# Norm sums by column in a kernel's closing stages, and products of half the tokens ahead of the other half's statistics

## The chip, the cores and the metric

The kernel runs on one core of one Trainium2 chip. The metric is the time of one execution on the device in microseconds (us), less being better. Its engines are TensorE (PE, with its weight loads as PEld), VectorE (DVE), ScalarE (ACT), GpSimd (POOL) and SyncE (SP); each works through its own queue of instructions in order, and semaphores tie the queues together.

## The reference: what is computed

Two layers over 256 latent tokens `x_l` and 256 context tokens `x_c`, 1024 wide, in float32. Each layer normalises, mixes tokens by four branches, adds, normalises again, and runs a feed-forward network with a short convolution over the tokens:

```python
def rmsnorm(x, g):
    xf = x.astype(jnp.float32)
    y = xf * lax.rsqrt(jnp.mean(xf * xf, axis=-1, keepdims=True) + NORM_EPS)
    return (y * g.astype(jnp.float32)).astype(x.dtype)

def modulate(h, shift, scale):
    return h * (1.0 + scale) + shift

def conv_ffn(h, p):
    u = dwconv(h @ p['w_up'], p['ffn_conv_w'], p['ffn_conv_b'], (FFN_CONV - 1) // 2)
    g, v = jnp.split(u, 2, axis=-1)
    return (jax.nn.silu(g) * v) @ p['w_down']

def layer(x_l, x_c, c, c_ctx, p, cos, sin, lambda_init, with_ctx_out):
    mod_l = (jax.nn.silu(c) @ p['w_ada'] + p['b_ada'])[:, None, :]
...
    h_l = modulate(rmsnorm(x_l, p['norm1_g']), sh1_l, sc1_l)
    h_c = modulate(rmsnorm(x_c, p['norm1_g']), sh1_c, sc1_c)
    y_l, y_c = token_mixer(h_l, h_c, p, cos, sin, lambda_init, with_ctx_out)
    x_l = x_l + g1_l * y_l
    x_l = x_l + g2_l * conv_ffn(modulate(rmsnorm(x_l, p['norm2_g']), sh2_l, sc2_l), p)
    if not with_ctx_out:
        return x_l, None
...
```

In the second layer the context tokens end after the mixer's keys and values; its last stages work on the latent tokens alone. The result is `x_l`.

## The kernel before

**Layout.** The tokens stand as columns: `x` is `xm` [128, 8, 512], eight blocks ("columns" below, k or j) of 128 of the 1024 features by 512 tokens; tokens 0 to 255 are the latent ones (`v` = 0), 256 to 511 the context ones (`v` = 1).

**Products.** Each factor is split into a high and a low part (`Mat`, `split`, L253): ScalarE or VectorE makes the high part (a cast, L256), VectorE or GpSimd subtracts it to get the low part (L251). A product is three TensorE matmuls (`mm3`, L267 to L269: low x high, high x low, high x high). The text ahead counts such matmuls, each 128x256 or 128x512, when it says "products". `fm` (L525) runs k over the eight columns for one tile of 128 outputs; with `halves` it does the context tokens first, then the latent ones. Results lie in PSUM in four buffers `big` and four `small`.

**Weights** are loaded by SyncE's queue (`wcols`, `wraw`) into two buffers, and split into four buffers `whl`. `turn[1]` says whose turn it is for the low part: GpSimd every `turn[1]`th time, VectorE else; `NEVER` keeps it on VectorE.

**A norm.** `norm_stats` (L497) squares each column on ScalarE (L503, L506) and adds the squares up on VectorE (L507). `rstd` (L477) sums over the partitions by two small matmuls with ones (L484), scales on VectorE (L487), takes the power -1/2 on GpSimd (L489), and spreads the result over the partitions by two matmuls (L493). `norm` (L511) then makes `h` column by column: times the broadcast (L517, VectorE), scale and shift (L519 ScalarE for odd columns, L521 VectorE for even ones), and the split into `hh` (ScalarE, L256) and `hl` (L251, VectorE for every fourth column, GpSimd else). The temporary `fo` has three buffers. The scale and shift come from `norm_coeffs` (L455).

**Closing stages.** `closing` (L1107) makes the last product of a mixer ("out") or of a feed-forward network ("down3") for four columns at a time, context tokens first, and adds it to `x` (L1119). A norm of `x` follows at three places, called A, B and C from here on: A, the end of layer 0's mixer into `norm2` and the products `up0` and `up1`; B, the end of layer 0's feed-forward network into `norm1` of layer 1 and the products `rgx0` and `rgx1` (`rg_in`, L989); C, the end of layer 1's mixer (latent tokens alone) into `norm2` and `up0`.

**Filler.** While layer 0's feed-forward network runs, a `Filler` (L411) makes layer 1's modulation: 48 blocks of weights `wa` are loaded by ScalarE's queue into two buffers, multiplied by the conditioning row `crow` and summed, for the latent vector on VectorE (L435), for the context one on GpSimd (L431) and ScalarE (L432). `crow` itself is made by `cond` (L291 to L303). The filler is handed out in shares between the feed-forward tiles.

**What sets the order.** The Python code emits the instructions; a planner then places them in each engine's queue by simulated time, within the dependences. `tc.high_priority()` puts what is emitted inside it ahead of what is ready at the same time; `tc.issue_after(i)` keeps what is inside from being placed before instruction `i`. `after[l, j0]` (L1120) holds the last residual update of a half of a closing stage for that use.

Of the kernel before, what the change touches and what calls it, by code (L numbers as in the profile page):

```python
# [14 lines left out]
OP = mybir.AluOpType  # L15
# [192 lines left out]
def _build(ctx, nc, tc, I, out, dbg):  # L208
# [56 lines left out]
    def mm3(ps, a, b, start, stop):  # L265

        PE.matmul(ps, a.l, b.h, start=start, stop=False)  # L267
        PE.matmul(ps, a.h, b.l, start=False, stop=False)  # L268
        PE.matmul(ps, a.h, b.h, start=False, stop=stop)  # L269
# [241 lines left out]
    def norm(x, rs, a, sh):  # L511
        h = Mat(*(hp.tile([128, KT, T], F32R, name=f"h{i}") for i in "hl"))
        for v, r in rs.items():
            ts = slice(v * 256, v * 256 + 256)
            for k in range(KT):
                t = tt("fo", 256)
                V.tensor_tensor(t, x[:, k, ts], r, op=OP.mult)  # L517
                if k % 2:
                    S.activation(t, t, AF.Identity, scale=a[:, k, v:v + 1], bias=sh[:, k, v:v + 1])  # L519
                else:  # L520
                    V.tensor_scalar(t, t, a[:, k, v:v + 1], sh[:, k, v:v + 1], op0=OP.mult, op1=OP.add)  # L521
                split(h[:, k, ts], t, V if k % 4 == 3 else G)
        return h

    def fm(ps, w, h, n, start=True, stop=True, halves=False):  # L525

        if halves and n > 256:
            for v in reversed(range(n // 256)):
                ts = slice(v * 256, v * 256 + 256)
                fm(ps[:, ts], w, h[:, :, ts], 256)  # L530
            return
        kn = w.h.shape[1]
        for k in range(kn):
            mm3(ps, w[:, k], h[:, k, :n], start and k == 0, stop and k == kn - 1)
# [20 lines left out]
    class Mixer:  # L555
# [433 lines left out]
        def rg_in(self, i, tag, bufs):  # L989

            l, p, h = self.l, self.p, self.h
            w = wcols(l, f"rgx{i}")
            xr = self.long([128, 2, T], tag, bufs)
            bws = []
            for c in range(2):
                cp = 2 * i + c
                ps = big()
                fm(ps, w[c], h, T, halves=True)
# [108 lines left out]
    def closing(l, name, acts, x, g, n, fill=None):  # L1107

        kn = len(acts)
        for j0 in range(0, 8, 4):  # L1110
# [12 lines left out]

    def ffn(l, p, x, h, n, last, fp, fill=None):
        def up(f0, f1):
            acts = []
            for i in range(f0, f1):
                turn[1] = NEVER if i < 2 else 2
                w = wcols(l, f"up{i}")
                o = []  # L1130
                for s in range(2):
                    ps = big(n)
                    fm(ps, w[s], h, n, halves=i < 2)
# [13 lines left out]
        def down(g, acts, fin):  # L1147
            f0, f1 = FGROUPS[g]
            if g == len(FGROUPS) - 1 and not fin:
                closing(l, f"down{g}_", acts, x, g2, n)  # L1150
                return
# [26 lines left out]
        down(len(FGROUPS) - 1, prev, last)  # L1178
# [54 lines left out]
    for l in range(DEPTH):  # L1233
        full = l < DEPTH - 1
        if l:
            p = load_params(l)
            with tc.high_priority():
                r = norm_stats(x, T)
        with tc.issue_after(after[0, 4]) if l else nullcontext():
            a1, sh1 = norm_coeffs(p, mods[l], 0, "norm1", 1, 2)  # L1240
        h = norm(x, r, a1, sh1)
# [8 lines left out]
        rin = [mx.rg_in(0, "bcm", 1), mx.rg_in(1, "xs", 2)]  # L1250
# [64 lines left out]
        closing(l, "out", ms, x, g1, n, fill and (lambda: fill.share(0.5)))  # L1315
# [6 lines left out]
        with tc.high_priority():  # L1322
            h = norm(x, norm_stats(x, n), a2, sh2)
# [5 lines left out]
        ffn(l, p, x, h, n, not full, fp, fill)  # L1329
# [17 lines left out]
```

## Time and profile before

| | |
|---|---|
| time, median of 3 runs (lowest to highest) | 1796.97 us (1796.64 to 1797.96) |
| the profiled execution | 1793.63 us, its span 1791.8 us |
| TensorE busy | 1695.5 us, 95% |
| VectorE, ScalarE, GpSimd busy | 68%, 52%, 48% |
| mean granted TensorE clock | 0.979 of full speed |

The span runs from the first to the last instruction; the rest of the profiled execution's time lies around it. Start times below are from the span's start. A timeline row has start, duration, engine and line, operation, tile written <- tiles read, and in brackets how long the engine stood idle before and what ended that. Matmuls overlap: the distance between two starts is the step, the second number is how long one takes from start to end. In windows, PEclk is the granted clock of TensorE, 1.00 being 2.4 GHz and 0.50 being 1.2 GHz.

### The profile page before, as it was taken

To read this page: it belongs to the slowest core of one execution; us is meant where nothing else is said; L and a number is where in the kernel's file an instruction comes from. 1 tells how busy PE (TensorE), PEld (TensorE's weight loads), DVE (VectorE), ACT (ScalarE), POOL (GpSimd) and SP (SyncE) were. 2 spreads that over 40 slices of the span, in tenths; PEclk is the share of its full clock that TensorE was granted. 3 is DMA by queue.
4 is the path that set the end of the run, shared out by engine and by line. 5 is a ranking of instruction groups with operands and counts; after the bars stand their busy time and mean duration, and the time that the engine had idled before them with its cause. 6 is when DMAs were issued, how large, how long until landed. Compare 5 with 4: busy or idle time off the path is not lost.

```text
span 1791.8 us, 27924 instructions
## 1 busy us (share of the span) xinstructions
PE 1695.5 (95%) x10758; PEld 1496.4 (84%) x10758; DVE 1216.4 (68%) x2185; ACT 927.7 (52%) x1697; POOL 859.2 (48%) x522
## 2 busy tenths in 40 slices
PE   7998999999899998999999999985999999989999
PEld 2966788889798787987778889865889999989998
DVE  6768766546877676898756475668775667567664
ACT  3456664554545444555534343465555555556554
POOL 4434664253436566567534332444673345434443
PEclk8999999999999999999999999998999999999999
DMA  7322433131313356435645443222333133445553
GB/s 297 101 80 72 130 106 107 60 107 48 118 72 121 106 168 243 154 133 186 207 168 178 136 160 106 88 94 95 103 134 118 48 119 118 169 152 191 188 184 129
DMA packets 52037, 237.10 MB, mean 132 GB/s; under 512 B 9664, under 2 KB 12608, under 8 KB 34496
## 3 DMA queue, kind: packets, MB, share of 16 engines
q1 hardware_dynamic: 28080, 179.46, 28.9%
q10 hardware_dynamic: 23824, 55.86, 9.7%
q8 instruction: 85, 1.39, 0.3%
q14 instruction: 48, 0.39, 0.1%
HBM read 234.18 MB, written 1.11 MB: 131 GB/s over the span
## 4 chain that ended last, share of the span: by engine, by line
PE 40%; DVE 4%; DMA 3%; ACT 3%; POOL 2%; issue 1%; ACTq 0%; POOLq 0%; SPq 0%
PE big L267 12%; PE big L268 12%; PE big L269 12%; DMA w<-in_w 2%; POOL whl L251 1%; ACT whl L256 1%; DMA wa<-in_w 1%; POOL wa L431 1%; PE small L589 1%; PE small L775 1%; DVE whl L251 1%; PE small L816 0%; PE small L625 0%; PE small L731 0%; PE small L732 0%
## 5 line engine op out<-in xcount | busy, mean ns | idle before, releaser
L251 POOL TENSOR_TENSOR whl<-w,whl 128x1024 fp32r<-128x1024 f32 (+3 forms) x194 | 451.7, 2331 | 497.7 <-ACT whl L256 462.4
L267 PE MATMUL big<-hh,whl 128*128 128x256 f32 (+1 forms) x1632 | 549.7, 341 | 21.8 <-DVE fo L552 14.2
L269 PE MATMUL big<-hh,whl 128*128 128x256 f32 (+1 forms) x1632 | 549.9, 338 | 0.0
L268 PE MATMUL big<-hl,whl 128*128 128x256 f32 (+1 forms) x1632 | 547.4, 337 | 0.8 <-POOL hl L251 0.8
L256 ACT CAST whl<-w 128x1024 fp32r<-128x1024 f32 (+3 forms) x342 | 334.2, 986 | 153.6 <-PE big L269 75.5
L267 PEld LDWEIGHTS big<-hh,whl 128*128 128x128 f32 x1632 | 311.8, 193 | 59.1 <-issue 20.3
L268 PEld LDWEIGHTS big<-hl,whl 128*128 128x128 f32 x1632 | 313.2, 192 | 34.0 <-issue 3.5
L269 PEld LDWEIGHTS big<-hh,whl 128*128 128x128 f32 x1632 | 313.0, 192 | 32.5 <-issue 3.2
L251 DVE TENSOR_TENSOR whl<-w,whl 128x1024 fp32r<-128x1024 f32 (+2 forms) x150 | 199.7, 1333 | 64.7 <-ACT whl L256 64.3
L552 DVE SCALAR_TENSOR_TENSOR fo<-big,pp,fo 128x510 f32<-128x510 f32 (+2 forms) x224 | 141.2, 634 | 70.7 <-ACT fo L544 67.5
L431 POOL TENSOR_TENSOR wa<-wa,crow 128x1024 f32<-128x1024 f32 x48 | 127.7, 2662 | 75.0 <-DVE fo L435 42.7
L268 PE MATMUL big<-whl,hh 128*128 128x256 f32 (+1 forms) x512 | 147.0, 287 | 1.7 <-POOL whl L251 1.7
L269 PE MATMUL big<-whl,hh 128*128 128x256 f32 (+1 forms) x512 | 147.4, 288 | 0.0
L267 PE MATMUL big<-whl,hl 128*128 128x256 f32 (+1 forms) x512 | 146.5, 287 | 0.7 <-ACT A L721 0.5
L267 PE MATMUL big<-act,whl 128*128 128x256 f32 (+1 forms) x392 | 126.0, 322 | 3.3 <-POOL whl L251 3.3
L269 PE MATMUL big<-act,whl 128*128 128x256 f32 (+1 forms) x392 | 125.8, 321 | 0.0
L268 PE MATMUL big<-act,whl 128*128 128x256 f32 (+1 forms) x392 | 125.2, 320 | 0.0
L544 ACT ACTIVATE fo<-big,pp 128x512 f32<-128x512 f32 (+1 forms) x104 | 71.1, 683 | 93.1 <-PE big L269 84.7
L267 PE MATMUL big<-bo,whl 128*128 128x512 f32 (+1 forms) x256 | 88.7, 350 | 20.7 <-ACT bo L256 13.0
L268 PEld LDWEIGHTS big<-whl,hh 128*128 128x128 f32 x512 | 97.9, 191 | 2.1 <-POOL whl L251 1.9
L267 PEld LDWEIGHTS big<-whl,hl 128*128 128x128 f32 x512 | 97.7, 191 | 1.6 <-ACT A L721 0.7
L269 PEld LDWEIGHTS big<-whl,hh 128*128 128x128 f32 x512 | 98.0, 191 | 0.0
(296 smaller groups left out, 3270.3 us busy)
## 6 DMA issues: line engine op xcount, KB each, us to landing
w<-in_w SPq DMA_DIRECT2D x136, 1024.0 KB, 4.9
wa<-in_w ACTq DMA_DIRECT2D x64, 512.0 KB, 3.5
w<-in_w SPq DMA_DIRECT2D x16, 768.0 KB, 4.4
w<-in_w SPq DMA_DIRECT2D x16, 640.0 KB, 3.9
bcm<-in_w ACTq DMA_DIRECT2D x14, 512.0 KB, 3.6
q<-csd ACTq DMA_DIRECT2D x24, 256.0 KB, 4.2
wa<-in_w SPq DMA_DIRECT2D x11, 512.0 KB, 8.4
xm<-in_xT ACTq DMA_DIRECT2D x8, 512.0 KB, 7.7
```

The lines of the kernel that those rows point to most:

```text
L251: eng.tensor_tensor(o, v, hi.bitcast(F32), op=OP.subtract)
L256: S.copy(m.h, v)
L267: PE.matmul(ps, a.l, b.h, start=start, stop=False)
L268: PE.matmul(ps, a.h, b.l, start=False, stop=False)
L269: PE.matmul(ps, a.h, b.h, start=False, stop=stop)
L431: G.tensor_tensor(w, w, cr, op=OP.mult)
L544: S.activation(o, ps, AF.Identity, scale=wt[:, nc_ + c:nc_ + c + 1], bias=b[:, c:c + 1])
L552: V.scalar_tensor_tensor(os_, is_, wt[:, j * nc_ + c:j * nc_ + c + 1], os_, op0=OP.mult, op1=OP.add)
L589: PE.transpose(ps[:, i * 128:(i + 1) * 128], s, ident)
L775: PE.matmul(ops[t][:, hd * 64:(hd + 1) * 64], et[:, kb * 128:(kb + 1) * 128], self.gv[:, k0 + kb, vs], start=kb == 0, stop=kb == kn - 1)
```

## The change

`closing` squares and adds up each column right behind its residual update, with high priority, and returns the statistics: for the context tokens `rstd` is run at once, for the latent tokens it is left as a function to call. `norm` gets a `front`: the weights of the next stage's first pair (`rgx0` or `up0`). Where a statistic is such a function, it issues the pair's products of the context tokens, and only behind the first of these the latent tokens' statistics. `rg_in` and `up` then add the latent half alone for that pair. The pair's low parts are made on VectorE. `norm_coeffs` of layer 1 may be placed earlier (after the first half of the closing stage), the weights `rgx1` after the last sum.

```diff
+                    with tc.high_priority():
+                        if v not in acc:
+                            acc[v] = tt("tg", 256, bufs=2)
+                            S.activation(acc[v], xs, AF.Square)
+                        else:
+                            sq = tt("sq", 256, bufs=2)
+                            S.activation(sq, xs, AF.Square)
+                            ins = V.tensor_tensor(acc[v], acc[v], sq, op=OP.add)
...
+                if j0 + 4 == 8:
+                    after["sum"] = ins.ins
+                    if v or n == 256:
+                        with tc.high_priority():
+                            rs[v] = next(rstd([acc[v]], 256, 1.0 / D))
+                    else:
+                        rs[v] = lambda: next(rstd([acc[0]], 256, 1.0 / D))
+        return rs
...
-    def norm(x, rs, a, sh):
+    def norm(x, rs, a, sh, front=None):
...
         for v, r in rs.items():
             ts = slice(v * 256, v * 256 + 256)
+            if callable(r):
+                front.ps = [big() for _ in front.w]
+                ins = [fm(ps[:, 256:], w, h[:, :, 256:], 256) for ps, w in zip(front.ps, front.w)]
+                with tc.high_priority(), tc.issue_after(ins[0].ins):
+                    r = r()
...
+                if front:
+                    ps = front.ps[c]
+                    fm(ps[:, 0:256], w[c], h, 256)
+                else:
+                    ps = big()
+                    fm(ps, w[c], h, T, halves=True)
...
         if l:
             p = load_params(l)
-            with tc.high_priority():
-                r = norm_stats(x, T)
-        with tc.issue_after(after[0, 4]) if l else nullcontext():
+        with tc.issue_after(after[0, 0]) if l else nullcontext():
             a1, sh1 = norm_coeffs(p, mods[l], 0, "norm1", 1, 2)
-        h = norm(x, r, a1, sh1)
+        front = None
+        if l:
+            turn[1] = NEVER
+            front = Front(wcols(l, "rgx0"))
+        h = norm(x, r, a1, sh1, front)
...
-        rin = [mx.rg_in(0, "bcm", 1), mx.rg_in(1, "xs", 2)]
+        rin = [mx.rg_in(0, "bcm", 1, front)]
+        with tc.issue_after(after["sum"]) if l else nullcontext():
+            rin.append(mx.rg_in(1, "xs", 2))
...
         with tc.high_priority():
-            h = norm(x, norm_stats(x, n), a2, sh2)
+            turn[1] = NEVER
+            front = Front(wcols(l, "up0")) if full else None
+            h = norm(x, r, a2, sh2, front)
```

`up` does for `up0` what `rg_in` does for `rgx0`. Every engine has the same number of instructions as before, SyncE's and ScalarE's transfers included; SyncE's order is the same, and so is that of all engines at C. What follows is the order at the places where it differs; numbers behind names tell buffers' tiles apart. Lines behind `norm` have moved in the changed kernel: L1136 is the residual update (L1119 before), L1145 the sum of squares (L507), L524 and L528 are L517 and L521.

TensorE at A, before: context products of the first tiles (`big_7283`, `big_7336`, `big_7418`), then the latent tokens' sums and at once their broadcast (statistics `rs_7168`), then more products. The first four behind the broadcast are context products, too.

```order
L268 MATMUL big_7336<-hl_7174,whl_7280 128x256
L269 MATMUL big_7336<-hh_7173,whl_7280 128x256
L268 MATMUL big_7418<-hl_7174,whl_7412 128x256
L269 MATMUL big_7418<-hh_7173,whl_7412 128x256
L484 MATMUL small_7163<-ones_92,tg_7140 128x1 x2
L493 MATMUL small_7170<-cst_90,rs_7168 128x128 x2
L267 MATMUL big_7283<-hh_7173,whl_7277 128x256
L267 MATMUL big_7336<-hh_7173,whl_7280 128x256
L267 MATMUL big_7418<-hh_7173,whl_7412 128x256
L267 MATMUL big_7471<-hh_7173,whl_7415 128x256
L268 MATMUL big_7471<-hl_7174,whl_7415 128x256
```

TensorE at A, changed: the last of the 96 context products of all four tiles (`up0`, `up1`), the broadcast (`rs_7268`), and the first latent products, which read what that broadcast goes into.

```order
L269 MATMUL big_7471<-hh_7171,whl_7415 128x256
L267 MATMUL big_7471<-hh_7171,whl_7415 128x256
L268 MATMUL big_7471<-hl_7172,whl_7415 128x256
L269 MATMUL big_7471<-hh_7171,whl_7415 128x256
L493 MATMUL small_7270<-cst_90,rs_7268 128x128 x2
L267 MATMUL big_7213<-hh_7171,whl_7165 128x256
L267 MATMUL big_7214<-hh_7171,whl_7168 128x256
L267 MATMUL big_7418<-hh_7171,whl_7412 128x256
L267 MATMUL big_7471<-hh_7171,whl_7415 128x256
L268 MATMUL big_7213<-hl_7172,whl_7165 128x256
L269 MATMUL big_7213<-hh_7171,whl_7165 128x256
```

The sums stand 18 products ahead of this broadcast, behind 78 context products; before, 27 context products stood ahead of the sums and none between sums and broadcast.

VectorE at B, before, right behind the last residual update: parts of scale and shift, the first normalising of context columns, a weight's low part (another stands ahead of that update), and the last sums ahead of the first scaling (L521).

```order
L465 TENSOR_TENSOR A1_10154<-mod1_97,pp_10084 128x8
L464 TENSOR_TENSOR sh1_10155<-mod1_97,pp_10084 128x8
L465 TENSOR_TENSOR A1_10154<-mod1_97,pp_10084 128x8
L517 TENSOR_TENSOR fo_10164<-xm_6620,small_10118 128x256
L517 TENSOR_TENSOR fo_10169<-xm_6620,small_10118 128x256
L517 TENSOR_TENSOR fo_10174<-xm_6620,small_10118 128x256
L251 TENSOR_TENSOR whl_10417<-w_10412,whl_10417 128x1024
L507 TENSOR_TENSOR tg_10121<-tg_10121,sq_10138 128x256
L471 TENSOR_TENSOR g2_15873<-mod1_97,pp_10084 128x16
L466 SCALAR_TENSOR_TENSOR A1_10154<-A1_10154,pp_10084 128x8 x2
L507 TENSOR_TENSOR tg_10121<-tg_10121,sq_10141 128x256
L521 TENSOR_SCALAR fo_10164<-fo_10164,A1_10154,sh1_10155 128x256
```

VectorE at B, changed: both last updates, a sum, the normalising, the first scaling, the last sum, and two weights' low parts.

```order
L1145 TENSOR_TENSOR tg_9891<-tg_9891,sq_10096 128x256
L1136 SCALAR_TENSOR_TENSOR xm_6620<-big_10099,g2_7889,xm_6620 128x256
L1136 SCALAR_TENSOR_TENSOR xm_6620<-big_10119,g2_7889,xm_6620 128x256
L1145 TENSOR_TENSOR tg_9891<-tg_9891,sq_10116 128x256
L524 TENSOR_TENSOR fo_10162<-xm_6620,small_10056 128x256
L524 TENSOR_TENSOR fo_10167<-xm_6620,small_10056 128x256
L524 TENSOR_TENSOR fo_10172<-xm_6620,small_10056 128x256
L471 TENSOR_TENSOR g2_15873<-mod1_97,pp_10140 128x16
L528 TENSOR_SCALAR fo_10162<-fo_10162,A1_10144,sh1_10145 128x256
L1145 TENSOR_TENSOR tg_9891<-tg_9891,sq_10136 128x256
L251 TENSOR_TENSOR whl_10414<-w_10412,whl_10414 128x1024
L251 TENSOR_TENSOR whl_10417<-w_10412,whl_10417 128x1024
```

Scale and shift are made some 20 instructions earlier, and the first scaling has moved ahead of the weights' low parts and the last sum. On TensorE at B the latent tokens' sums stood right behind the context broadcast, ahead of any product, and their broadcast four products later; now 76 context products stand ahead of these sums and 20 more ahead of the broadcast, as at A.

GpSimd in the feed-forward stage behind A, before: filler multiplies (`wa`) and weights' low parts (`whl`).

```order
L431 TENSOR_TENSOR wa_7396<-wa_7396,crow_7265 128x1024
L251 TENSOR_TENSOR whl_7548<-w_7543,whl_7548 128x1024
L431 TENSOR_TENSOR wa_7398<-wa_7398,crow_7265 128x1024
L251 TENSOR_TENSOR whl_7633<-w_7628,whl_7633 128x1024
L431 TENSOR_TENSOR wa_7404<-wa_7404,crow_7265 128x1024
L431 TENSOR_TENSOR wa_7531<-wa_7531,crow_7265 128x1024
L251 TENSOR_TENSOR whl_7718<-w_7713,whl_7718 128x1024
L431 TENSOR_TENSOR wa_7537<-wa_7537,crow_7265 128x1024
L431 TENSOR_TENSOR wa_7616<-wa_7616,crow_7265 128x1024
L251 TENSOR_TENSOR whl_7809<-w_7804,whl_7809 128x1024
```

GpSimd there, changed.

```order
L431 TENSOR_TENSOR wa_7396<-wa_7396,crow_7323 128x1024
L251 TENSOR_TENSOR whl_7548<-w_7543,whl_7548 128x1024
L251 TENSOR_TENSOR whl_7633<-w_7628,whl_7633 128x1024
L431 TENSOR_TENSOR wa_7398<-wa_7398,crow_7323 128x1024
L431 TENSOR_TENSOR wa_7404<-wa_7404,crow_7323 128x1024
L251 TENSOR_TENSOR whl_7718<-w_7713,whl_7718 128x1024
L431 TENSOR_TENSOR wa_7531<-wa_7531,crow_7323 128x1024
L431 TENSOR_TENSOR wa_7537<-wa_7537,crow_7323 128x1024
L251 TENSOR_TENSOR whl_7809<-w_7804,whl_7809 128x1024
```

`whl_7633` has moved ahead of one multiply, `whl_7718` ahead of one, `whl_7809` ahead of one, later ones ahead of up to two; the last two of these weights (`whl_8392`, `whl_8442`) have 20 and 22 multiplies ahead of them in both.

## Rows read from the trace of the kernel before

**Rows 1.** The page, part 1: busy time and share of the span by engine.
```profile
PE 1695.5 (95%) x10758; PEld 1496.4 (84%) x10758; DVE 1216.4 (68%) x2185; ACT 927.7 (52%) x1697; POOL 859.2 (48%) x522
```

**Rows 2.** Timeline of TensorE at A: start, us, engine line op tiles, [idle before <-releaser].
```profile
749.76 0.50 PE L484 MATMUL small<-ones,tg 128*128 128x1 f32 x4
752.20 0.71 PE L493 MATMUL small<-cst,rs 128*128 128x128 f32 x4 [1.94 <-POOL rs L489]
...
753.94 0.42 PE L267 MATMUL big<-hh,whl 128*128 128x256 f32 x1
754.15 0.41 PE L268 MATMUL big<-hl,whl 128*128 128x256 f32 x1
...
774.03 0.40 PE L267 MATMUL big<-hh,whl 128*128 128x512 f32 x1
```

**Rows 3.** Windows: length, then busy us (instructions) of each engine; PEclk, DMA share, GB/s.
```profile
752.65:756.06 3.41, 3.41 (x19) 3.41 (x18) 2.93 (x8) 1.51 (x4) 2.25 (x4) 0.53 0.85 306
756.10:774.00 17.90, 17.90 (x150) 17.90 (x150) 13.37 (x26) 11.82 (x21) 6.95 (x7) 1.00 0.00 1
900.00:910.00 10.00, 7.69 (x26) 6.18 (x27) 2.83 (x6) 4.46 (x7) 6.45 (x4) 0.83 0.39 138
```

**Rows 4.** Timeline of VectorE and ScalarE at A, latent columns to first convolution.
```profile
752.87 0.76 DVE L517 TENSOR_TENSOR fo<-xm,small 128x256 f32<-128x256 f32 x2 [0.94 <-POOL hl L251]
...
762.60 0.42 DVE L251 TENSOR_TENSOR hl<-fo,hh 128x256 fp32r<-128x256 f32 x1
...
765.87 0.69 DVE L303 SCALAR_TENSOR_TENSOR crow<-fo,crow 128x512 f32<-128x512 f32 x1
768.04 0.78 ACT L544 ACTIVATE fo<-big,pp 128x512 f32<-128x512 f32 x1 [3.75 <-PE big L269]
768.93 0.75 DVE L552 SCALAR_TENSOR_TENSOR fo<-big,pp,fo 128x510 f32<-128x510 f32 x1 [2.37 <-ACT fo L544]
```

**Rows 5.** Waits in 769 to 860: waiter <- releaser: us in total, times, longest.
```profile
POOL wa L431 <- DVE fo L435: 27.6, 12, 8.6
...
DVE fo L435 <- DMA wa<-in_w: 5.9, 6, 2.0
...
PE big L267 <- POOL whl L251: 2.1, 2, 1.4
```

**Rows 6.** Waits of TensorE in 840 to 905; timeline at its last, GpSimd and TensorE.
```profile
PE big L267 <- POOL whl L251: 5.4, 4, 2.8
898.12 2.38 POOL L431 TENSOR_TENSOR wa<-wa,crow 128x1024 f32<-128x1024 f32 x1 [4.83 <-DMA wa<-in_w]
902.31 0.51 PE L267 MATMUL big<-act,whl 128*128 128x512 f32 x1 [2.81 <-POOL whl L251]
```

**Rows 7.** Timeline of TensorE, the queue of ScalarE and VectorE at B.
```profile
1122.91 0.28 PE L269 MATMUL big<-act,whl 128*128 128x256 f32 x1
...
1123.31 1.30 ACTq L1005 DMA_DIRECT2D q<-in_rgw  x2
...
1127.76 0.73 DVE L521 TENSOR_SCALAR fo<-fo,A,sh 128x256 f32<-128x256 f32 x2
1127.90 0.67 PE L484 MATMUL small<-ones,tg 128*128 128x1 f32 x4 [4.27 <-DVE tg L507]
1128.66 1.22 PE L267 MATMUL big<-hh,whl 128*128 128x256 f32 x4
...
1153.67 0.29 PE L267 MATMUL big<-whl,hl 128*128 128x272 f32 x1
```

**Rows 8.** Timeline of TensorE and VectorE at C.
```profile
1591.77 0.71 PE L493 MATMUL small<-cst,rs 128*128 128x128 f32 x4 [1.04 <-POOL rs L489]
1592.52 1.08 DVE L517 TENSOR_TENSOR fo<-xm,small 128x256 f32<-128x256 f32 x3 [1.59 <-PE small L493]
...
1594.42 1.22 PE L267 MATMUL big<-hh,whl 128*128 128x256 f32 x4 [1.94 <-ACT hh L256]
...
1599.77 0.42 DVE L251 TENSOR_TENSOR hl<-fo,hh 128x256 fp32r<-128x256 f32 x1 [1.11 <-ACT hh L256]
```

More of the change, by code (lines that the diff above doesn't have):

```diff
@@ L268, in mm3 @@
         PE.matmul(ps, a.h, b.l, start=False, stop=False)
-        PE.matmul(ps, a.h, b.h, start=False, stop=stop)
+        return PE.matmul(ps, a.h, b.h, start=False, stop=stop)
     def xtile():
@@ L523, in norm, with __init__ @@
         return h
+    class Front:
+        def __init__(self, w):
+            self.w, self.ps = w, None
     def fm(ps, w, h, n, start=True, stop=True, halves=False):
@@ L533, in fm @@
         for k in range(kn):
-            mm3(ps, w[:, k], h[:, k, :n], start and k == 0, stop and k == kn - 1)
+            ins = mm3(ps, w[:, k], h[:, k, :n], start and k == 0, stop and k == kn - 1)
+        return ins
     def tm(ps, w, t, h):
@@ L1109, in closing @@
         kn = len(acts)
+        acc, rs = {}, {}
         for j0 in range(0, 8, 4):
@@ L1120, in closing, with ffn @@
                     after[l, j0] = ins.ins
+                    with tc.high_priority():
[6 more added lines that the diff above has]
+                            ins = V.tensor_tensor(acc[v], acc[v], sq, op=OP.add)
                     if fill is not None and j0 == 0:
                         fill()
-    def ffn(l, p, x, h, n, last, fp, fill=None):
+                if j0 + 4 == 8:
[6 more added lines that the diff above has]
+        return rs
+    def ffn(l, p, x, h, n, last, fp, fill=None, front=None):
         def up(f0, f1):
@@ L1128, in up @@
                 turn[1] = NEVER if i < 2 else 2
-                w = wcols(l, f"up{i}")
+                ahead = front and i == 0
+                w = front.w if ahead else wcols(l, f"up{i}")
                 o = []
                 for s in range(2):
-                    ps = big(n)
-                    fm(ps, w[s], h, n, halves=i < 2)
+                    if ahead:
+                        ps = front.ps[s]
+                        fm(ps[:, 0:256], w[s], h, 256)
+                    else:
+                        ps = big(n)
+                        fm(ps, w[s], h, n, halves=i < 2)
                     c = tt("fo", n)
@@ L1149, in down @@
             if g == len(FGROUPS) - 1 and not fin:
-                closing(l, f"down{g}_", acts, x, g2, n)
-                return
+                return closing(l, f"down{g}_", acts, x, g2, n)
             for j in range(8):
@@ L1177, in ffn @@
             fill.finish()
-        down(len(FGROUPS) - 1, prev, last)
+        return down(len(FGROUPS) - 1, prev, last)
     def opened(name, bufs=1):
@@ L1314, in _build @@
         g1 = gate_coeffs(p, mods[l], 16, 0.5, 1)
-        closing(l, "out", ms, x, g1, n, fill and (lambda: fill.share(0.5)))
+        r = closing(l, "out", ms, x, g1, n, fill and (lambda: fill.share(0.5)))
         if fill:
@@ L1328, in _build @@
                           lambda i, v: v == 1 or i >= 16 and i % 2 == 0)
-        ffn(l, p, x, h, n, not full, fp, fill)
+        r = ffn(l, p, x, h, n, not full, fp, fill, front)
         closed(qf)
```

6 lines of the change are left out of this document (2 added, 4 removed).

## The prediction

> **What bounds the kernel now.** I read the page first: TensorE is busy for 95% of the span [rows 1]. A change in the order of work can therefore pay only where TensorE stands still or runs at half clock, and cost only by making more of either. A measurement of this kernel can tell about 0.2% (3.6 us) from no change.
>
> Next I read TensorE's stretches around the three places where a closing stage hands over to a norm. At **A** (layer 0, into norm2) TensorE ends its products of the context tokens, computes the sums of the latent tokens at 749.76, stands idle for 1.94 us until their broadcast at 752.20, and then issues products 0.21 us apart (753.94 to 754.15) [rows 2]; from 756.10 on 150 pass in 17.90 us, 0.12 each. The granted clock is 0.53 in the 3.41 us before that, 1.2 GHz for nearly all of them, and 1.00 behind [rows 3]: 3.41 / 0.213 is 16 products, which at 0.12 take 1.5 us less. At **B** (layer 0, into norm1 of layer 1) it idles 4.27 us between the context tokens' broadcast and the latent tokens' sums, and the first product starts at 1128.66 [rows 7]. At **C** (layer 1, into norm2, latent tokens alone) 2.65 us pass from the broadcast to the first product [rows 8].
>
> Between A and B lies the first feed-forward stage with its filler work. There I read the waits: no wait of VectorE, ScalarE or GpSimd in 769 to 860 is ended by a product; the longest are GpSimd's multiply waiting for VectorE's filler line, 27.6 us in 12 waits, and VectorE waiting for filler weights [rows 5]. TensorE itself waits four times, 5.4 us in all, for a weight's low part from GpSimd; the last is 2.81 us before 902.31, and the GpSimd multiply ahead of that weight had itself waited 4.83 us for its transfer [rows 6]. So this stretch ends when the filler's chain (transfer, VectorE, GpSimd, ScalarE, two buffers) lets it end, not when TensorE could.
>
> **The change, part by part.** Every engine and both DMA queues have as many instructions as before; the order alone changes. The squares and sums were already taken as columns came free, so summing in the closing loop removes no work. At C the order of all engines is the same: 0.
>
> *A, TensorE.* 51 more context products now stand ahead of the sums, 18 more ahead of the broadcast, and none is left behind it. At 0.12 us each the sums come at 749.76 + 51 x 0.12 = 755.9. From sums to broadcast took 2.44 us here (749.76 to 752.20) [rows 2], more than the 18 products' 2.2; so the broadcast is at 758.3, and the old gap of 1.94 shrinks to about 0.2. But nothing covers what follows: the normalising of the first latent column. C shows that: 2.65 us from broadcast to product [rows 8]. First latent product: 760.9. 96 remain, 16 at 0.213 and 80 at 0.12 (13.0 us): 773.9, against 774.03 before. For TensorE A is worth nothing: the gap is moved behind the broadcast. If the clock stays up, 11.5 us, and it is 1.6 us ahead.
>
> *A, the vector chain.* This decides, since TensorE is not what ends the next stretch. VectorE began the latent columns at 752.87 and ended them with the low part at 762.60 (0.42); the conditioning row's pieces then ran to 765.87 + 0.69 = 766.6, and the first convolution began at 768.93 [rows 4]. Now the latent columns begin at 758.3 + 0.75 (C: 1591.77 to 1592.52) = 759.1. The eight columns of C took 7.7 us (1592.52 to 1599.77 + 0.42) [rows 8]; those of A 10.15 (752.87 to 763.02), with context columns still in the way. After them 3.5 us of row pieces: 770.3 or 772.7. The first tile ends 59 products after the first latent one, at 760.9 + 3.4 + 5.2 = 769.5, and its convolution on VectorE follows 0.9 later, behind ScalarE's part (768.04 to 768.93): 770.4. So convolution and first filler come 1.4 to 3.8 us late. I take 1.8, near the row of C, because now as there no context column is left. GpSimd's pace here is not safe.
>
> *Feed-forward, layer 0.* Eight weights move ahead of one or two filler multiplies in GpSimd's queue. That can remove the first two stalls, 2.1 us of the 5.4 [rows 5, 6]. But the two narrow weights behind the last two stalls have 20 and 22 multiplies ahead of them, as before; if the filler ends 1.8 us later, so does the last weight, and TensorE waits there for what it gained. Term: +1.8. Bounds: -7.1 at the lower end (all 5.4 us go, and with them the low clock of 0.83 in 900 to 910, 3.4 us at half rate, 1.7 us [rows 3]), +3.8 at the upper.
>
> *B.* The last closing product ends at 1122.91 + 0.28 = 1123.2. The first context column's scale came only at 1127.76, behind two weights' low parts and the last sums, and for it the first product waited until 1128.66 [rows 7]. Now both weights stand behind that scale. VectorE then has one update and one sum, 0.9 us together, ahead of the normalising: 1124.1; by C's 1.90 us from there to the product (1592.52 to 1594.42) [rows 8] the first product could start at 1126.0. ScalarE allows less: its square of the last column (0.4), two transfers of `rgw` at 0.65 (two in 1.30 [rows 7]), an odd column's scale (0.6), one more transfer and the cast (0.4) stand ahead of the product: 1123.7 + 3.4 = 1127.1, 1.6 earlier than before. Then 76 context products, 16 of them slow, 10.6 us: 1137.7; sums to broadcast 2.44, hidden by 20 products: 1140.1; again 2.65 us with nothing to do: 1142.8; 96 latent products in 13.0: 1155.8. Before, the next kind of product began at 1153.67: **+2.1**. One gap has become two. If the clock stays up after the second, +0.6; if the transfers cost ScalarE no time either, -0.5; if the columns come at A's pace and the sums 1 us late, +3.1. What follows is a run of TensorE's own products, so it is not hidden there.
>
> *Layer 1.* The planner also orders some 600 products of the mixer differently, with the same numbers. I know no sign for it: 0, with one stall of the largest kind seen, 2.8 us [rows 6], as the bound on either side.
>
> Sum: 0 + 1.8 + 2.1 = **+3.9 us**. On the profiled execution, 1793.63 us, that is 1797.5; the median of the runs, 1796.97, is 3.3 us above it and gives **1800.9 us**.
>
> [...] Rows 2 and 3 show that after an idle time of 1.94 us, with short sums and broadcasts around it, products ran at 1.2 GHz. [...] No row of this kernel has a lone gap of that length between dense products.
>
> **The rivals.**
> 1. *Faster: GpSimd's new order is what counts.* The stalls for weights vanish, because TensorE's weights no longer stand behind multiplies that wait for transfers. For it: the four stalls are all of this kind [rows 6]. Against it: the filler's length [rows 5] and the unchanged place of the last weights. It decides if the filler's chain has at least 1.8 us to spare at 902. All of it: -7.1 + 2.1 = -5.0, 1792.0 us; the first two stalls and the clock alone: -3.8 + 2.1 = -1.7.
> 2. *No change that can be told.* The second gaps don't cost clock (-0.5 to +0.6 at B), and the filler hides part of A's delay, or all (0 to +1.8). 1796.5 to 1799.4 us. For it: half clock at A was seen where short sums and broadcasts stood beside the gap [rows 2, 3], and VectorE has 5.9 us of idle time while it waits for filler weights [rows 5]. Against it: at the second gaps a broadcast stands beside the gap, too.
> 3. *Slower than forecast.* Column work goes at A's pace, not C's, since VectorE's and GpSimd's instructions lengthen each other: +3.8 at A and +3.1 at B, 1803.9 us. It decides if a latent column takes 1.27 us instead of 0.96.
> 4. *The change does not do what it says:* at C it does nothing, and the sums by column were in the order before. That is in every case above.
>
> **How the numbers follow.** Forecast 0.40, rival 1 0.25, rival 2 0.22, rival 3 0.13. The forecast lies just beyond the bound of 3.6 us, so of its chance 0.24 is slower and 0.16 the same. Rival 1 gives 0.19 faster and 0.06 the same; rival 2 is the same but for 0.02 on the slow side; rival 3 is slower. Together: faster 0.19, same 0.42, slower 0.39. The range goes from rival 1's better part, 1792.5, to rival 3 with part of the unknown of layer 1, 1806.
>
> **What the profile after would show.** Right: at A no idle time ahead of the broadcast, but about 1.9 us behind it, and half clock after that; first convolution on VectorE some 2 us later than 768.9; the last stall for a weight at 902 still there and later; at B a first product near 1127.1, a second gap near 1140, and the first 272-wide product near 1156; at C the same gaps as before. Wrong: products behind the second gaps at 0.12 us (then rival 2), TensorE without waits for GpSimd's weights between 840 and 905 (then rival 1), or a filler that ends at the old time although it began late.

## The result, and the profile after

The changed kernel took 1808.28 us (median of four, 1807.46 to 1813.14) against 1796.94 us beside it: a ratio of 1.0073, 95% interval 1.0059 to 1.0087. That is 11 us by the medians and 13 us by the ratio, slower and beyond the range that was given. The profiled execution, 1813.14 us, is the longest of the four, so the starts below are some 3 us late before the change has done anything; differences within one stretch are what counts.

TensorE is as busy as before, 1700.7 us against 1695.5 [rows 1]; the time went into waits.

```profile
PE 1700.7 (94%) x10758; PEld 1499.3 (83%) x10758; DVE 1218.8 (67%) x2185; ACT 928.1 (51%) x1697; POOL 864.4 (48%) x522
```

**A and the stretch behind it.** The timeline of TensorE in the changed kernel (columns as in [rows 2]):

```profile
741.36 0.58 PE L484 MATMUL small<-ones,tg 128*128 128x1 f32 x4 [1.06 <-DVE tg L1145]
...
746.01 0.60 PE L493 MATMUL small<-cst,rs 128*128 128x128 f32 x4
...
760.39 0.50 PE L484 MATMUL small<-ones,tg 128*128 128x1 f32 x4
...
762.99 0.60 PE L493 MATMUL small<-cst,rs 128*128 128x128 f32 x4
765.60 0.74 PE L267 MATMUL big<-hh,whl 128*128 128x256 f32 x4 [2.01 <-ACT hh L256]
...
779.10 0.47 PE L267 MATMUL big<-hh,whl 128*128 128x512 f32 x1 [1.40 <-ACT whl L256]
...
826.11 0.47 PE L267 MATMUL big<-hh,whl 128*128 128x512 f32 x1 [1.69 <-DVE fo L564]
...
840.99 0.77 PE L267 MATMUL big<-hh,whl 128*128 128x512 f32 x1 [3.75 <-DVE fo L564]
...
915.84 0.80 PE L267 MATMUL big<-act,whl 128*128 128x512 f32 x1 [4.17 <-POOL whl L251]
```

Ahead of the latent broadcast (762.99) there is no idle time any more, and behind it there are 2.01 us. From there on the forecast of A holds: 2.61 us from broadcast to product, where 2.65 was taken. One wait is new and was not in the forecast: 1.06 us ahead of the context tokens' sums, for the last of the sums by column. The traces of all seven executions that sum by column at A have it, 0.51 to 1.07 us long; the other seven have none. The 512-wide products start 33.1 us behind the context tokens' broadcast (746.01 to 779.10). Before it was 32.2, by a row not shown so far (the first of these; the others are GpSimd's first filler multiplies and weights, same view):

```profile
741.80 0.60 PE L493 MATMUL small<-cst,rs 128*128 128x128 f32 x4
...
770.90 3.33 POOL L431 TENSOR_TENSOR wa<-wa,crow 128x1024 f32<-128x1024 f32 x1 [8.65 <-DVE fo L435]
774.20 3.38 POOL L251 TENSOR_TENSOR whl<-w,whl 128x1024 fp32r<-128x1024 f32 x1
777.54 3.37 POOL L431 TENSOR_TENSOR wa<-wa,crow 128x1024 f32<-128x1024 f32 x1
```

From the 512-wide products to the one that follows the last long wait for a weight took 128.3 us before (774.03 to 902.31, [rows 2, 6]); now it takes 136.7 (779.10 to 915.84). **These 8.5 us are the largest piece.** TensorE stands still for VectorE's convolutions where it hardly did before (1.69 and 3.75 us are the longest), and longer for the last weight (4.17 against 2.81). VectorE's first convolution comes 29.3 us behind the context broadcast (746.01 to 775.27) instead of 27.1 (741.80 to 768.93, [rows 4]). The timelines of VectorE and of GpSimd in the changed kernel show how the stretch begins:

```profile
775.27 0.74 DVE L564 SCALAR_TENSOR_TENSOR fo<-big,pp,fo 128x510 f32<-128x510 f32 x1
...
777.23 3.31 POOL L431 TENSOR_TENSOR wa<-wa,crow 128x1024 f32<-128x1024 f32 x1 [6.34 <-DVE fo L435]
780.50 6.70 POOL L251 TENSOR_TENSOR whl<-w,whl 128x1024 fp32r<-128x1024 f32 x2
787.16 2.41 POOL L431 TENSOR_TENSOR wa<-wa,crow 128x1024 f32<-128x1024 f32 x1
```

Two weights in a row take 6.70 us, and the second multiply comes 9.9 us after the first (777.23 to 787.16); before, with one weight between them, it was 6.6 (770.90 to 777.54). A buffer goes free when ScalarE has summed what this multiply writes, and the next filler transfer needs it. So VectorE waits for transfers: in 775 to 900, by the view of waits (columns as in [rows 5]), first before, then changed:

```profile
ACT wa L432 <- POOL wa L431: 26.6, 13, 3.9
...
DVE fo L435 <- DMA wa<-in_w: 10.0, 8, 2.4
...
ACT small L1138 <- DVE fo L552: 4.7, 4, 2.6
```

```profile
ACT small L1176 <- DVE fo L564: 23.8, 8, 5.6
...
DVE fo L435 <- DMA wa<-in_w: 18.0, 12, 2.9
ACT wa L432 <- POOL wa L431: 13.5, 11, 2.6
...
PE big L267 <- DVE fo L564: 6.9, 4, 3.7
```

VectorE works in order, so the convolutions that stand behind a waiting filler instruction wait with it, and TensorE waits for the PSUM buffers that these would free: 6.9 us.

ScalarE's waits have turned round as well: it waits half as long for GpSimd's multiplies (13.5 us instead of 26.6) and five times as long for VectorE's convolutions (23.8 instead of 4.7). ScalarE also issues the filler's transfers, so what holds it up holds them up. The orders of VectorE and ScalarE in this stretch differ from before, too, which the list of places in "The change" leaves out. GpSimd's order is therefore not the only candidate for the loss.

**B.** The timeline of TensorE in the changed kernel:

```profile
1137.38 0.28 PE L269 MATMUL big<-act,whl 128*128 128x256 f32 x1
...
1140.70 1.33 PE L267 MATMUL big<-hh,whl 128*128 128x256 f32 x3 [2.59 <-ACT hh L256]
1143.16 0.58 PE L268 MATMUL big<-hl,whl 128*128 128x256 f32 x1 [1.14 <-POOL hl L251]
...
1153.85 0.50 PE L484 MATMUL small<-ones,tg 128*128 128x1 f32 x4
...
1156.68 0.60 PE L493 MATMUL small<-cst,rs 128*128 128x128 f32 x4
1159.30 0.74 PE L267 MATMUL big<-hh,whl 128*128 128x256 f32 x4 [2.01 <-ACT hh L256]
...
1172.73 0.29 PE L267 MATMUL big<-whl,hl 128*128 128x272 f32 x1
```

From the last closing product to the first 272-wide one: 35.35 us (1137.38 to 1172.73) against 30.76 (1122.91 to 1153.67, [rows 7]), so 4.6 us are lost. The first product does come earlier, 3.3 us behind the closing stage instead of 5.75. But the first low part of `h` is awaited for 1.14 us, the sums come 13.15 us behind the first product, and behind the broadcast there is a gap of 2.01 us. VectorE and GpSimd at that wait:

```profile
1140.17 2.35 DVE L251 TENSOR_TENSOR whl<-w,whl 128x1024 fp32r<-128x1024 f32 x2
...
1140.72 3.82 POOL L251 TENSOR_TENSOR hl<-fo,hh 128x256 fp32r<-128x256 f32 x3 [2.07 <-ACT hh L256]
```

While VectorE makes the two low parts of `rgx1`, GpSimd needs 3.82 us for three low parts of `h`: 2.39 for the first, for which TensorE waits, and some 0.75 for each of the others, as at C. The windows of TensorE (columns as in [rows 3]) show the clock behind the gaps:

```profile
765.60:770.60 5.00, 4.92 (x39) 4.71 (x40) 3.08 (x8) 3.94 (x10) 4.04 (x6) 1.00 0.00 0
1140.70:1145.00 4.30, 3.17 (x11) 2.62 (x12) 3.96 (x7) 1.47 (x4) 3.82 (x3) 0.50 0.54 129
1145.00:1148.00 3.00, 3.00 (x19) 3.00 (x18) 1.96 (x5) 2.43 (x7) 1.51 (x3) 0.61 0.39 137
1159.30:1161.30 2.00, 1.92 (x13) 1.72 (x14) 0.89 (x3) 1.27 (x4) 1.98 (x3) 0.92 0.00 0
1161.30:1164.30 3.00, 3.00 (x16) 3.00 (x16) 2.19 (x6) 2.56 (x7) 2.06 (x4) 0.50 0.02 5
```

Behind the gap at A it stayed at 1.00; behind the first one at B it was 0.50 for 4.3 us and 0.61 in the 3 us after that, and behind the second it fell only after some 1.7 us of products (0.92 on average in the first 2.0). C is as before: idle times of 2.88, 1.04 and 1.94 us ahead of sums, broadcast and first product.

### The profile page after: what moved, and what is told of

It reads as the page before. It is cut to its first block, busy times and chain, and to the rows that moved or that the text cites. A ratio compares the mean times of both kernels' runs of the same rounds, so it can differ in the third digit from the quotient of the medians.

```text
span 1811.3 us, 27924 instructions
## 1 busy us (share of the span) xinstructions
PE 1700.7 (94%) x10758; PEld 1499.3 (83%) x10758; DVE 1218.8 (67%) x2185; ACT 928.1 (51%) x1697; POOL 864.4 (48%) x522
## 4 chain that ended last, share of the span: by engine, by line
PE 42%; DVE 5%; ACT 3%; DMA 2%; POOL 2%; issue 1%; ACTq 0%; DVEq 0%; POOLq 0%; SPq 0%
PE big L267 13%; PE big L268 13%; PE big L269 13%; DMA wa<-in_w 1%; DMA w<-in_w 1%; ACT whl L256 1%; POOL whl L251 1%; DVE fo L564 1%; PE small L601 1%; PE small L787 1%; PE small L828 0%; ACT wa L432 0%; DVE whl L251 0%; DVE fo L435 0%; PE small L743 0%
## 5 line engine op out<-in xcount | busy, mean ns | idle before, releaser
L267 PE MATMUL big<-bo,whl 128*128 128x512 f32 (+1 forms) x256 | 88.5, 350 | 21.5 <-ACT bo L256 13.0
```

## The experiments

Each stands beside runs of the kernel before on its chip; microseconds are its ratio less 1 times 1796. Two theories were set against each other first. **Q**: GpSimd's new order, weights ahead of multiplies, holds up the filler, which sets the end of the feed-forward stage. **S**: the late start of the latent columns at A does it. For B: **G**, the second gap, and **H**, the first spell behind the closing stage.

**1. A alone.** `closing`, `norm_coeffs` and `rg_in` at B as before:

```diff
-            return closing(l, f"down{g}_", acts, x, g2, n)
+            return closing(l, f"down{g}_", acts, x, g2, n, cols=False)
...
-        h = norm(x, r, a1, sh1, front)
+        h = norm(x, norm_stats(x, T), a1, sh1)
```

> The change at A alone (closing of layer 0's mixer into norm2 and up0), B as before. The profile of the change puts about 9 to 11 us between the end of that mixer and the end of layer 0's feed-forward stage, and 4.5 us at B. Both theories (GpSimd's order, or the late start of the latent columns) expect +6 to +9 us against the kernel before, so 1803 to 1806; a theory by which B carries the loss expects +2 or less.

Measured: 1.0040 (1.0027 to 1.0054), +7.2 us. It has the changed kernel's GpSimd order in the feed-forward stage. More than half of the loss is made at A or in the stretch behind it; B is the lesser part.

**2. B alone.** The same at A: `norm(x, norm_stats(x, n), a2, sh2)`, and `closing` of layer 0's mixer without sums.

> The change at B alone (closing of layer 0's feed-forward network into norm1 and rgx0), A as before. By the gaps in the profile of the change (first product 2.4 us earlier, a second gap of 2.0 us, half clock behind both): +3 to +5 us. The prediction's term was +2.1. If the planner's other order of layer 1's mixer matters, the time is off these values and the offset grows behind 1165 us.

Measured: 1.0018 (1.0007 to 1.0030), +3.2 us, with the two gaps of the changed kernel, 2.59 us ahead of the first product and 2.00 behind the latent broadcast.

**3 and 4. GpSimd's order by itself, in both directions.** Each weight's low part on GpSimd is queued behind a given number of filler multiplies, and the next multiply behind it:

```diff
+    COUNTS = [1, 2, 4, 6, 9, 11, 14, 16, 17, 19, 20, 22]
...
+            with tc.issue_after(f.gs[c - 1]):
+                split(m, v, eng, V if turn[0] % turn[2] == 0 else None)
```

These are the numbers of the kernel before, put into the changed kernel:

> The changed kernel, with GpSimd's queue in layer 0's feed-forward stage held to the order it had before (each weight's low part behind as many filler multiplies as before). Theory Q (weights ahead of multiplies hold up the filler): 7 to 8 us come back, +3 to +5 us against before, TensorE's stalls for VectorE's convolutions near 826 and 841 vanish. Theory S (the late start at A is what counts): no more than 1 us comes back, +10 to +12.

Measured: 1.0039 (1.0024 to 1.0053), +7.0 us instead of +13, between the two theories' ranges and nearer to Q's. And the numbers of the changed kernel (1, 1, 3, 5, 7, 9, 12, 14, 17, 18, 20, 22) put into the kernel before:

> The kernel before, with GpSimd's queue in layer 0's feed-forward stage held to the order of the changed kernel; nothing at A or B differs from before. Theory Q: +5 to +8 us, lost between 775 and 905. Theory S: within 1 us of before. The prediction's first rival (stalls for weights vanish): 2 to 5 us faster.

Measured: 1.0028 (1.0015 to 1.0040), +5.0 us, with nothing of the change at A or B. The waits in 775 to 900, first of this kernel, then of the changed one with the order of before:

```profile
DVE fo L458 <- DMA wa<-in_w: 16.7, 13, 3.4
...
PE big L269 <- DVE fo L587: 6.3, 4, 3.0
```

```profile
DVE fo L458 <- DMA wa<-in_w: 6.6, 6, 2.2
...
PE big L269 <- DVE fo L587: 1.5, 2, 1.0
```

The new order brings VectorE's waits for transfers (16.7 us) and TensorE's waits for convolutions (6.3), and taking it back removes them. The stretches from the first 512-wide product to the last long wait say the same, by TensorE's timelines of these two kernels:

```profile
775.99 0.40 PE L269 MATMUL big<-hh,whl 128*128 128x512 f32 x1
...
910.50 0.50 PE L269 MATMUL big<-act,whl 128*128 128x512 f32 x1 [2.86 <-POOL whl L253]
```

```profile
781.17 0.47 PE L269 MATMUL big<-hh,whl 128*128 128x512 f32 x1 [0.49 <-DVE fo L587]
...
908.75 0.79 PE L269 MATMUL big<-act,whl 128*128 128x512 f32 x1 [2.47 <-POOL whl L253]
```

134.5 and 127.6 us, where the kernel before took 128.3. All traces agree: the eight with GpSimd's order of before have 126.8 to 130.6 us here, the four with the changed order 133.6 to 137.5. S falls, since the order costs 5.0 us with nothing changed at A, and the forecast's first rival, by which this order would free TensorE, has the wrong sign.

Q is shown only in part. Where GpSimd's order was set, the planner moved VectorE's and ScalarE's instructions in this stretch along with it: in experiment 4 near to their order in the changed kernel (ScalarE waits 21.5 us for convolutions), in experiment 3 near to that of before (5.2 us). So the order of this stretch costs the time, but whether GpSimd's weights ahead of multiplies do it, or what moved along on the other two engines, is not shown: GpSimd's order with theirs unchanged was not tried.

**5. The other way round.** One more multiply ahead of each weight than in the kernel before (2, 3, 5, 7, 10, 12, 15, 17, 18, 20, 21, and the last as it was).

> The kernel before, with each of GpSimd's weights in the feed-forward stage behind one more filler multiply than before, the other way round from the change. Theory Q (a weight ahead of a multiply holds up the filler, which sets the end): 1 to 3 us faster, VectorE's waits for filler transfers below 10 us, and if the weights then come too late, TensorE's waits for them above 5.4 us and no gain. Theory R (GpSimd's order is no cause, the planner's other order of VectorE and ScalarE is): no telling, between -3 and +5.

Measured: 1.0015 (1.0004 to 1.0027), +2.7 us: a miss for the gain, while the bound that the expectation named came true. The waits in the same window:

```profile
PE big L269 <- POOL whl L253: 8.3, 4, 3.4
...
DVE fo L458 <- DMA wa<-in_w: 5.1, 5, 2.1
```

VectorE's waits for transfers fall from 10.0 to 5.1 us, and TensorE waits 8.3 us for weights instead. The order of before lies between two losses (VectorE's and ScalarE's order moved along here, too).

**6. One weight alone** moved ahead of one multiply (1, 1, 4, 6, ...).

> The kernel before, with one weight alone (the second of GpSimd's in the feed-forward stage) moved ahead of one filler multiply. Theory Q: the first multiplies come 3 us later, as in the changed kernel (two weights in a row took 6.7 us there), and if nothing gives that back, +2 to +3 us; if the later order gives it back, 0. Theory R: within 1 us.

Measured: 1.0004 (0.9994 to 1.0015), no difference. By its trace the second multiply comes 9.97 us after the first, as in the changed kernel, and the sixth is back in its old place, counted from the first 512-wide product. So the two weights in a row at the head are not by themselves what costs the time; how many swaps it takes was not tried.

**7. A without GpSimd's order.** Experiment 1 with the counts of experiment 3.

> The change at A alone with GpSimd's order of before in the feed-forward stage: what A costs by itself. The prediction's term (latent columns and filler start late): +1.8 us. By the difference of two earlier runs (changed kernel with GpSimd's order of before, +7.0, less B alone, +3.2): +3.8 us. Theory Q needs it well below the +7.2 of A with its own GpSimd order.

Measured: 1.0011 (1.0001 to 1.0020), +2.0 us, in size the term that the forecast put at +1.8. Its feed-forward stretch takes 127.3 us (775.79 to 903.13), no more than before. Where the 2.0 us lie is not shown, because the profiled execution, 1793.03 us, is the fastest of the twelve and 4.9 us below their median. It has both candidates, VectorE's first convolution 2.1 us later behind the context broadcast and a wait of 0.51 us ahead of the context tokens' sums.

**8. Sums by column alone**, both halves' statistics at once, no product moved:

```diff
+                r = {v: q() if callable(q) else q for v, q in r.items()}
...
-        h = norm(x, r, a1, sh1, front)
+        h = norm(x, r, a1, sh1)
```

> Sums by column in the closing stages alone: both halves' statistics are computed at once, no product is moved ahead of them. The prediction held that this part removes and adds nothing: within 1 us of before. The rival: the context sums at A come 1 us later, as in the changed kernel (1.06 us of idle time ahead of them): +1 us.

Measured: 1.0016 (1.0005 to 1.0026), +2.9 us. Both expectations miss. TensorE at B:

```profile
1128.06 1.01 PE L484 MATMUL small<-ones,tg 128*128 128x1 f32 x4 [3.92 <-DVE tg L1146]
1130.10 1.22 PE L493 MATMUL small<-cst,rs 128*128 128x128 f32 x4 [1.03 <-POOL rs L489]
```

The latent broadcast now stands ahead of any product and is awaited for 1.03 us. In [rows 7] four products stood between sums and broadcast. At A the context tokens' sums are awaited for 0.59 us, which the kernel before did not do. The forecast held that summing by column adds nothing; by the time it does, and 0.59 us of that stand at A. That the wait at B costs anything is not shown: from the last closing product to the first 272-wide one B takes 32.4 us here, and 30.8 to 32.4 in the traces with B's closing stage as before (experiments 1 and 4 to 7, and the kernel before). Where the rest of the 2.9 us (0.9 to 4.7) lies stays open.

**9. The second gap at B covered.** The change at B alone, with statistics allowed from the third column on:

```diff
-            ins = mm3(ps, w[:, k], h[:, k, :n], start and k == 0, stop and k == kn - 1)
+            last = mm3(ps, w[:, k], h[:, k, :n], start and k == 0, stop and k == kn - 1)
+            ins = last if k <= 2 else ins
```

> The change at B alone, but the latent tokens' statistics may be placed from the third column of the first tile on instead of behind its last product: 34 context products (4.1 us) stand behind their broadcast. Theory G (the second gap of 2.0 us and the half clock behind it make B's loss): 2 to 3.5 us less than the change at B alone, so -0.5 to +1.5 us against before, and no idle time between the broadcast and the first latent product. Theory H (the first spell, with its wait for the first low part of h and half clock, makes the loss): +2 to +4.

Measured: 1.0005 (0.9996 to 1.0013), +0.9 us, 2.3 less than B alone. TensorE's timeline:

```profile
1121.75 0.28 PE L269 MATMUL big<-act,whl 128*128 128x256 f32 x1
...
1127.53 0.58 PE L268 MATMUL big<-hl,whl 128*128 128x256 f32 x1 [1.33 <-POOL hl L251]
...
1136.49 0.60 PE L493 MATMUL small<-cst,rs 128*128 128x128 f32 x4
...
1152.53 0.29 PE L267 MATMUL big<-whl,hl 128*128 128x272 f32 x1
```

No idle time follows the broadcast at 1136.49, and B takes 30.8 us (1121.75 to 1152.53), as before. The intervals of this run and of B alone overlap, but the traces say the same: B takes 35.0 to 36.5 us in the four executions that leave the second gap open (the changed kernel twice, experiments 2 and 3) and 29.5 to 32.1 us in the three that cover it (experiments 9 to 11). So G is most of B's loss. The wait for the first low part, 1.33 us, is still there.

**10. That wait removed, too.** Statistics from the fourth column on, and the low parts of `rgx1` behind VectorE's last low part of the context columns:

```diff
+                if v == 1 and k == 7:
+                    after["n1"] = lows[0]
...
-        with tc.issue_after(after["sum"]) if l else nullcontext():
+        with tc.issue_after(after["n1"]) if l else nullcontext():
```

> The change at B alone with the latent statistics from the fourth column on, and the low parts of rgx1's weights on VectorE behind the last low part of the context columns, so that no weight runs beside GpSimd's first low parts of h. Theory H2 (VectorE's two weights beside them stretch these from 0.75 to 1.27 us and make the wait of 1.1 to 1.3 us and a longer spell of half clock): 1 to 2 us less than with the early statistics alone, -1.5 to 0 us against before, and the wait for the first low part at 0.5 us or less. If the two weights then come too late for their own products: +0 to +2.

Measured: 0.9990 (0.9980 to 0.9999), 1.8 us faster than the kernel before, a little more than expected: the one version that beats both kernels, by 0.1%, with an interval that ends just short of no difference.

```profile
1119.91 0.28 PE L271 MATMUL big<-act,whl 128*128 128x256 f32 x1
...
1130.38 0.60 PE L495 MATMUL small<-cst,rs 128*128 128x128 f32 x4
...
1149.41 0.29 PE L269 MATMUL big<-whl,hl 128*128 128x272 f32 x1
```

B takes 29.5 us (1119.91 to 1149.41), and the wait for the first low part is 0.30 us. That is 1.03 of the 1.3 us between the two traces, so the first spell had a share as well (H2). One thing moved with it and was not tried apart: the statistics stand earlier here, with 58 context products behind their broadcast instead of 34.

**11. All of it with the better places.** The changed kernel with GpSimd's order of before, and statistics from the fourth column on at A and B.

> The changed kernel with GpSimd's order of before in the feed-forward stage, and the latent statistics from the fourth column of the first tile on, at A and at B: 24 context products stand behind each broadcast. That kernel without the earlier statistics was 7.0 us above before. Theory G: both second gaps of 2.0 us go, with what half clock follows them: +1 to +4 us. Theory H: +5 to +8.

Measured: 1.0031 (1.0019 to 1.0042), +5.6 us. Against the +7.0 of experiment 3 that is no difference that the intervals can tell, and it lies in H's range, a miss for G. Its trace has both gaps covered: 31.4 us instead of 33.7 from the context broadcast at A to the first 512-wide product, and 32.1 instead of 35.1 at B. But the feed-forward stretch takes 130.6 us instead of 127.6, so what A gave did not reach the end of that stretch.

**12. The whole again.**

> The changed kernel again, with the order of every engine as it was, beside before on one chip, to set the sum of the parts against the whole: A without GpSimd's order +2.0, GpSimd's order +5.0 to +6.3, B +3.2, together +10.2 to +11.5 us. If the parts are all there is, the whole is within 2 us of that; the first measurement gave a ratio of 1.0073 (+13). In its profile, stable features should come again: VectorE's waits for filler transfers near 18 us, two gaps of 2.0 us behind the broadcasts, a first product 3.2 us behind the broadcast at B; half clock behind the second gaps may come or stay away.

Measured: 1.0083 (1.0057 to 1.0108), +15 us (10 to 19). The parts, +10.2 to +11.5, lie within that interval, and 2 to 5 us may come from their meeting; that stays open. Its trace has the two gaps of 2.01 us and B at 35.0 us again; VectorE waits 15.2 us for transfers, less than the 18 expected, and the feed-forward stretch takes 133.6 us.

## Why the prediction was wrong

The sign was right, and not by luck, since the terms at A and B have it in the runs, too; its chance was the second highest of three. The size was wrong: +3.9 forecast, range up to +9, +11 to +13 measured.

- **C, 0:** right; its gaps are as before.
- **A, TensorE, 0, and the vector chain, +1.8:** right in size. Broadcast, gap and late first convolution (2.1 us) came as worked out, and A without GpSimd's new order costs +2.0 (experiment 7, 0.2 to 3.6). Left out was the wait of 0.51 to 1.07 us ahead of the context tokens' sums: the sums by column were held to move nothing, and alone they cost +2.9 (experiment 8).
- **Feed-forward, "Eight weights move ahead of one or two filler multiplies ... Term: +1.8": this step failed.** It priced the new order as something that could only gain, the two stalls of 2.1 us, and set the rest to the late start. Put into the kernel before, the new order of this stretch costs +5.0 us, and taking it out of the changed kernel gives back 6 (experiments 4 and 3). The text had part of the facts: the filler ends this stretch, by two buffers. It asked what the weights gain by going first and not what the multiplies lose, when each low part takes 2.4 to 3.4 us ahead of them. It also read the waits too narrowly: in 769 to 860 ScalarE waits 14.9 us for GpSimd's multiplies and 13.3 for VectorE, both longer than the 5.9 us of VectorE that it names, and how VectorE's and ScalarE's orders change here was not priced. Which of the three engines' orders makes the loss stays open. The upper bound, +3.8, left this out, and so the range was too short.
- **B, +2.1:** the mechanism, one gap made into two, was right, and the size off: +3.2 by the runs (1.3 to 5.4), 4.6 in the profile. The first product came earlier than worked out (3.3 us behind the closing stage, 4.2 forecast). The mis-sized term is the spell from the first product to the sums: 10.6 forecast, 13.15 measured. A second idle time of 1.14 us, for the first low part, came into it, and half clock lasted 6.8 us instead of 3.4. The idle time, 1.14 to 1.33 us, comes in every execution of the change at B as it stands; the longer half clock does not (experiment 12 has 3.4 us, and 12.7 from the first product to the sums).
- **Layer 1, 0:** nothing was found there. From the 272-wide products to the end both profiles take 638 us (1153.67 to 1791.8, and 1172.73 to 1811.3).
- **The rivals:** the first had its place right and its sign wrong; the third, columns at A's pace, did not come at A (VectorE's latent columns began 0.7 us behind the broadcast and took 8.1 us, where C took 7.7 and A before 10.15), though what it named, VectorE and GpSimd lengthening each other, showed in the first low part at B. Whether the clock stays up behind a second gap the forecast left open (+2.1 or +0.6 at B); both were seen, as told below.

## What to carry to other kernels

Where a chain of transfers with few buffers sets the end of a stage, ask of every reordering what it puts ahead of the instruction that frees the buffer: that side can have a price even where the instruction moved ahead is wanted sooner. Moving independent work ahead of a wait turns one gap into two when it is spent to the last product; here it paid, by 0.1%, only where some of it was kept for behind the second broadcast. And a scheduler that is given one new constraint may move what stands a hundred microseconds away, so the order of all engines is read before the time is forecast, and each difference priced with both signs. An experiment that holds one engine's order is subject to the same: compare the others' orders before the result is put down to that engine.

## What the runs showed of the hardware

**The clock behind a short gap.** Six executions of kernels with uncovered latent statistics hold nine gaps of 2.0 us between a broadcast and full-width products, with dense products ahead. Behind three of them the granted clock stayed at 1.00, behind six it fell to 1.2 GHz, and not at once: in the second execution of the changed kernel at A (windows as above) it was 0.94 in the first 2 us of products and 0.50 in the next 3.

```profile
762.60:764.60 2.00, 1.93 (x13) 1.72 (x14) 0.90 (x3) 1.28 (x4) 1.98 (x3) 0.94 0.00 0
764.60:767.60 3.00, 3.00 (x16) 3.00 (x16) 2.19 (x6) 2.67 (x7) 2.05 (x4) 0.50 0.00 0
```

At the same gap of the first execution it stayed up. So a gap of this length costs 0 or about 1.5 us (an estimate: 16 products at 0.213 us instead of 0.12), and the same kernel at the same place had either. The forecast had this as a choice between two cases. The first spell at B varies in the same way: experiment 6 has the instruction order of the kernel before there, but half clock lasted 6.8 us instead of 3.4, and B took 32.1 us instead of 30.8.

**GpSimd beside VectorE.** At the head of the feed-forward stage two low parts of weights took GpSimd 3.38 and 3.36 us, beside filler and weight instructions of VectorE, and 2.40 later; VectorE's own low part took 3.41 us there and 1.22 just before. The first low part of `h` at B took 2.39 us beside two of VectorE's low parts, and 0.73 in experiment 10, where these had been moved away and TensorE's wait fell from 1.33 to 0.30 us. The Trainium skill ("GPSIMD Engine Reference", Specifications) has the two engines share their SBUF interfaces and contend where VectorE reads two inputs from SBUF; the traces agree.
